# Moving the second query half's compressed softmaxes apart, and a side product behind the items' transposes, in an NSA layer

## The chip, the cores and the metric

The kernel runs on one core of one Trainium2 chip. The time is device microseconds of one execution of the whole program, as the median of several runs. Times inside the program come from one execution that the hardware profiler recorded. Its engines are TensorE (PE), VectorE (DVE), ScalarE (ACT), GpSimd (POOL) and SyncE (SP).

## The reference

A trunk of four layers over 256 tokens of width 1024, all in float32: differential attention, NSA (sparse attention with compressed, selected and window branches), forgetting attention, differential attention again; each layer also has a squared-ReLU MLP and a gated per-layer embedding. The part that matters here is layer 1, the NSA layer:

```python
s_c = einsum('bqgrd,bngd->bgrqn', qc, kc) * scale + b_c     # compressed branch, n_cmp = 15 blocks
p_c = masked_softmax(s_c, m_c)
o_c = einsum('bgrqn,bngd->bqgrd', p_c, vc)
...
s_s, s_w = ...     # scores against the selected and the window keys, 256 of each
p_s, p_w = masked_softmax(s_s, m_s), masked_softmax(s_w, m_w)
return gc[..., 0:1] * o_c + gc[..., 1:2] * o_s + gc[..., 2:3] * o_w
...
x = x + sigmoid(x @ ple_gate_w[i]) * (p[i] @ ple_w[i])      # the embedding; p[i] @ ple_w[i] needs nothing of the layer
```

There are 16 heads in 4 groups. The compressed softmax works on 15 numbers per head and token, so its operations are small, and they form a chain.

## The kernel before, in words

Attention in the NSA layer is cut into 16 **items** `(ap, t, j)`: `ap` is a pair of groups, `t` one of the two token halves of 128, `j` a pair of heads. The order of the items is the table `ORDN`; they are called item 0 to item 15 here. An item has two stages.

- First stage: two score matmuls in two `acc` banks of PSUM (L1005; each shows as two instructions, so a pair is x4), then per row block bias and minimum on DVE (L497), exp on ACT (L501).
- Second stage, three items later (`DP[1]` is 3): on DVE a reciprocal (L1011), the gate (L1013) and four scalings of the probabilities (L1022); on PE transposes into two `wk` banks (L1025), which ACT copies out (L1027), and products with the values into a `pj` bank (L1034), which a matmul with zeros opens where a new `(ap, t)` begins (L1016).

Between the items, `fill(n)` issues other work as the table `FILL` says; it runs after item n-1 has been started and item n-4 has been finished. The letters that matter:

- `s10`: the first part of the compressed softmax of group pair 1, token half 0; `s11` likewise for half 1, and so `s01`, `s00`. It is four small matmuls into a `wk` bank (L959), then a chain: DVE adds the bias (L962 twice), finds the minimum (L966) and subtracts it (L967), ACT takes exp (L968), DVE sums (L970), inverts (L971), applies the gate (L972), and multiplies into `pc` (L976).
- `t00`, `t01`, ...: its second part, four transposes (L982) and a copy by ACT (L983).
- `p`: one step of the embedding's product `ple_proj`: six matmuls of 512 columns in an `acc` bank (L173, L174, L175 twice each) and a copy by ACT (L1145). It depends on nothing in the layer.

Code is written in this order, and a scheduler turns it into one list for each engine; each engine then takes its own list strictly in order. `self.after(x)` holds what is written inside it until `x` stands in the lists. The four `acc` banks are shared by the scores and the embedding; the bias tiles `nb` (two buffers, L486, loaded through ACT's queue) of group pair 1 can be loaded when the last items of pair 0 have used theirs.

Of the kernel before, what the change touches and what calls it, by code (L numbers as in the profile page):

```python
# [18 lines left out]
P = 128  # L19
# [14 lines left out]
PACC = {0: 1, 1: 1, 2: 1, 3: 1}  # L34
PCB = 2
CW = 2
FILL = {-2: 'q0.c.p.q0.c', 1: 'p.g', 2: 'd0.q1.s01.d1', 3: 's00', 4: 't00.q1', 5: 's10.p.s11', 6: 'p', 7: 't01', 11: 't11.t10.O', 16: 'p'}
NORM = {0: 1, 1: 2, 2: 3, 3: 3}
MEP = 1
BANKS = dict(acc=('acc', 4), pj=('pj', 2), wk=('wk', 2))  # L40
# [40 lines left out]
def backwards(v):  # L81

    *rest, (step, n) = [list(z) for z in v.ap]
    return bass.AP(tensor=v.tensor, offset=v.offset + step * (n - 1), ap=[*rest, [-step, n]])


class Trunk:
# [756 lines left out]
    def nsa(self, i, hT):  # L844
        nc, a = self.nc, self.a
# [20 lines left out]
        for t in range(2):  # L866
# [13 lines left out]
            pt = self.wk()  # L880
# [8 lines left out]
        def fill(n):  # L889
            for z in FILL.get(n, "").replace(".", " ").split():  # L890
                if z[0] == "c":
                    if "ph" not in cmp:
                        cmp["ph"] = self.cpsum()
                        cmp["up"] = self.compress_up(blks, cmp["ph"])
                    next(cmp["up"])
                elif z[0] == "g":
                    cmp["hid"] = self.compress_gelu(cmp["ph"])
                elif z[0] == "d":
                    self.compress_down(int(z[1]), cmp["hid"], (kcT, vcd)[int(z[1])])
                elif z[0] == "s":  # L900
                    soft2[z[1:]] = cmp_soft(int(z[1]), int(z[2]), qt[int(z[1])])
                    next(soft2[z[1:]])
                elif z[0] == "t":
                    next(soft2[z[1:]])
                    soft2[z[1:]] = None
                elif z[0] == "q":
                    next(qs[int(z[1])])
                elif z[0] == "p":
                    next(self.ple)
                elif z[0] == "Q":  # L910
                    q_load(int(z[1]))
                elif z[0] == "O":
                    self.early.append(self.unit(self.w_out, len(self.early), 1, 0, D))
            if n > 0:
                for ap, t in last:
                    if (ap, t) in po4 and soft2.get(f"{ap}{t}", 1) is None and n >= last[ap, t] + DP[i]:
                        finish(ap, t)

        qt, po4, soft2 = {}, {}, {}
        last = {(z[0], z[1]): n + 1 for n, z in enumerate(ORDN)}  # L920
        cmp = {}
        blks = [self.compress_blocks(kind, kvT[:, 2 * kind : 2 * kind + 2, :]) for kind in range(2)]
# [4 lines left out]
        def q_load(ap):  # L927
            if ap in q_ws:
                return
            src = w_in[:, 512 * ap : 512 * ap + 512].rearrange("(c p) n -> p c n", p=P)  # L930
            us = q_ws[ap] = []
            for k in range(0, KD, 2):
                w = self.raw(src[:, k : k + 2, :], [4, 4, HD])
                us.append(self.split(w.rearrange("p k r d -> p r k d"), [4, 4, HD]))
# [18 lines left out]
        def cmp_soft(ap, t, qt):  # L953
# [30 lines left out]
            yield  # L984

        fill(-4)
        ksw = self.s4([P, 2, 2, S])
        for z, c in ((0, 512), (1, 1024)):
            o = self.lin_b(w_in, C0 + c, hT)
            nc.scalar.activation(ksw[:, :, z, :], o.rearrange("p (a b) -> p a b", a=2), AF.Copy)  # L990
            fill(z - 3)

        def item(ap, t, j, qt, nbs):


            nk = t + 1
            w = nk * P
            qs = slice(t * P, (t + 1) * P)
            sc = self.acc()
            es = self.es([P, 2, 2, w])  # L1000
            m, s = self.small([P, 4]), self.small([P, 4])
            rows = (j, j ^ 1)
            for g2, r in enumerate(rows):
                hs = slice(g2 * HD, (g2 + 1) * HD)
                nc.tensor.matmul(sc[g2][:, : 2 * w].rearrange("p (z k) -> p z k", z=2), qt[hs, r, qs], ksw[hs, ap, :, :w], start=True, stop=True)  # L1005
            for g2, r in enumerate(rows):
                zs = slice(2 * g2, 2 * g2 + 2)
                self.soft(es[:, g2], lambda b: sc[g2][:, b * w : (b + 1) * w], 2, lambda b: backwards(nbs[g2][:, r, :w]), m[:, zs], s[:, zs])
            for _ in range(DP[i]): yield
            rs = self.small([P, 2, 2])  # L1010
            nc.vector.reciprocal(rs.rearrange("p a b -> p (a b)"), s)  # L1011
            h0, h1 = 8 * ap + rows[0], 8 * ap + 4 + rows[1]
            nc.vector.tensor_tensor(rs, rs, gate[:, t, h0 : h1 + 1 : h1 - h0, 1:3], op=ALU.mult)  # L1013
            if (ap, t) not in po4:
                po4[ap, t] = self.pj()
                nc.tensor.matmul(po4[ap, t], self.zero[0:1, :], self.zero[0:1, 0:1].to_broadcast([1, 512]), start=True, stop=False)  # L1016
            ats = []
            for g2 in range(2):
                e = es[:, g2]
                pt = self.wk()  # L1020
                for z in range(2):
                    nc.vector.tensor_scalar(e[:, z, :], e[:, z, :], rs[:, g2, z : z + 1], None, op0=ALU.mult)  # L1022
                    for kb in range(nk):
                        zz = (z * nk + kb) * P
                        nc.tensor.transpose(pt[:, zz : zz + P], e[:, z, kb * P : (kb + 1) * P], self.ident)  # L1025
                at = self.m2([P, 2, nk, P])
                nc.scalar.activation(at.rearrange("p a b c -> p (a b c)"), pt[:, : 2 * w], AF.Copy)  # L1027
                ats.append(at)
            for z in range(2):
                for kb in range(nk):  # L1030
                    for g2, r in enumerate(rows):
                        g = 2 * ap + g2
                        ov = po4[ap, t][(r % 2) * HD : (r % 2 + 1) * HD, (2 * g2 + r // 2) * P : (2 * g2 + r // 2 + 1) * P]
                        nc.tensor.matmul(ov, vs[kb][:, z, g * HD : (g + 1) * HD], ats[g2][:, z, kb, :], start=False, stop=False)  # L1034

        def finish(ap, t):
            rows = slice(ap * HD, (ap + 1) * HD)
            for g2 in range(2):
                for r in range(4):
                    ov = po4[ap, t][(r % 2) * HD : (r % 2 + 1) * HD, (2 * g2 + r // 2) * P : (2 * g2 + r // 2 + 1) * P]  # L1040
                    nc.tensor.matmul(ov, vcd[rows, 2 * ap + g2, :], pcT[rows, t, r, :], start=False, stop=g2 == 1 and r > 1)
            self.split_out(po4.pop((ap, t)).rearrange("p (a b) -> p a b", a=4), oT, 4 * ap, 4, t)

        def fin():
            for _ in range(DP[i] - 1):
                yield
            fill(100)
            yield

        def items():  # L1050
            n = 0
            nbs = {}
            fill(-1)
            for ap, t, j in ORDN:
                if ap not in nbs:
                    nbs[ap] = [self.bias_load(8 * ap + 4 * g2) for g2 in range(2)]
                yield item(ap, t, j, qt[ap], nbs[ap])
                n += 1
                fill(n)
            yield fin()  # L1060
# [198 lines left out]
```

## Time and profile before

| what | value |
|---|---|
| median of 3 runs | 1384.98 us (1381.73, 1384.98, 1389.02) |
| profiled execution, its own time | 1391.75 us |
| its span, first to last instruction | 1390.0 us |
| PE busy | 1370.6 us, 99% |
| DVE, ACT busy | 906.8 us (65%), 756.9 us (54%) |
| mean granted TensorE clock | 0.991 |

A granted clock of 1.00 is 2.4 GHz and 0.50 is 1.2 GHz. PE is busy nearly all the time, so what PE waits, and what it does at the lower clock, is what a change of order can alter. The stage of the NSA items lies at about 423 to 490 us of the span.

### The profile page before, as it was taken

The page shows a single profiled execution, that of the slowest core. Times are in us where ns is not written, and L with a number is a line of the kernel's source. Part 1 is how long each engine was busy: PE and PEld are TensorE (multiplying, and loading weights), DVE is VectorE, ACT ScalarE, POOL GpSimd, SP SyncE. Part 2 cuts the span into 40 slices and gives each one's busy share as a digit, 9 for nine tenths or more (in the row PEclk, how much of TensorE's full clock was granted, in tenths as well). Part 3 has the DMA queues.
Part 4 walks back from the last instruction along what each step waited for, and adds up shares of the span by engine and source line. Part 5 has one row for each costly group of instructions (what it writes and reads, how often), then busy time and mean ns, then how long its engine had stood idle before and what let it go on. Part 6 is the DMA issues. An engine that isn't in the chain of part 4 may idle for free.

```text
span 1390.0 us, 20343 instructions
## 1 busy us (share of the span) xinstructions
PE 1370.6 (99%) x7604; PEld 1138.5 (82%) x7604; DVE 906.8 (65%) x1636; ACT 756.9 (54%) x1268; POOL 52.9 (4%) x101
## 2 busy tenths in 40 slices
PE   8999999999999999999999999999999999999998
PEld 6987888888875678888878978888888987888887
DVE  6677765667556657656584576766576677766655
ACT  5556554456445755554465575645456566554443
POOL 1011000001000000000010000000001011000000
PEclk9999999999998999999999999999999999999999
DMA  8845765646772036655366644656554753665642
GB/s 267 263 144 154 237 198 188 190 141 195 193 258 95 23 119 223 199 186 183 121 214 197 225 133 154 214 183 198 190 187 124 232 169 102 219 210 170 204 141 76
DMA packets 144526, 247.28 MB, mean 178 GB/s; under 512 B 10195, under 2 KB 101243, under 8 KB 144428
## 3 DMA queue, kind: packets, MB, share of 16 engines
q1 hardware_dynamic: 134848, 235.26, 52.7%
q10 hardware_dynamic: 9580, 10.73, 2.5%
q8 instruction: 60, 0.98, 0.3%
q14 instruction: 38, 0.31, 0.1%
HBM read 243.81 MB, written 1.10 MB: 176 GB/s over the span
## 4 chain that ended last, share of the span: by engine, by line
PE 88%; issue 5%; DVE 2%; ACT 2%; POOL 2%; DMA 1%; SPq 0%; DVEq 0%; POOLq 0%; ACTq 0%
PE pj L182 13%; PE acc L173 13%; PE acc L174 13%; PE acc L175 13%; PE pj L183 7%; PE pj L173 7%; PE pj L175 6%; PE pj L174 6%; PE wk L256 2%; PE acc L627 1%; PE pj L1034 1%; PE acc L1005 1%; PE wk L1025 1%; DMA raw<-in_da_w_in_dram 1%; DVE wl L151 1%
## 5 line engine op out<-in xcount | busy, mean ns | idle before, releaser
L151 DVE TENSOR_TENSOR wl<-raw,wh 128x1024 fp32r<-128x1024 f32 x421 | 510.4, 1221 | 226.7 <-ACT wh L150 215.1
L150 ACT ACTIVATE wh<-raw 128x1024 fp32r<-128x1024 f32 x421 | 443.2, 1058 | 225.5 <-PE acc L174 106.4
L182 PE MATMUL pj<-big,wh 128*128 128x512 f32 x768 | 274.3, 401 | 0.0
L183 PE MATMUL pj<-big,wl 128*128 128x256 f32 x768 | 215.5, 281 | 0.0
L173 PE MATMUL acc<-wh,s 128*128 128x512 f32 x512 | 200.3, 392 | 0.0
L175 PE MATMUL acc<-wl,s 128*128 128x512 f32 x512 | 199.4, 390 | 0.0
L174 PE MATMUL acc<-wh,s 128*128 128x512 f32 x512 | 199.3, 390 | 0.0
L182 PEld LDWEIGHTS pj<-big,wh 128*128 128x128 f32 x768 | 144.2, 188 | 38.2 <-DVE m L1079 3.5
L183 PEld LDWEIGHTS pj<-big,wl 128*128 128x128 f32 x768 | 145.0, 189 | 0.9
L173 PE MATMUL pj<-big,wh 128*128 128x256 f32 x480 | 138.2, 288 | 0.5 <-ACT wh L150 0.5
L174 PE MATMUL pj<-big,wl 128*128 128x256 f32 x480 | 137.0, 285 | 0.5 <-DVE wl L151 0.5
L175 PE MATMUL pj<-big,wh 128*128 128x256 f32 x480 | 137.1, 286 | 0.0
L173 PE MATMUL acc<-wh,big 128*128 128x512 f32 (+2 forms) x344 | 131.6, 383 | 2.3 <-ACT wh L150 2.3
L174 PE MATMUL acc<-wh,big 128*128 128x512 f32 (+2 forms) x344 | 130.7, 380 | 0.0
L175 PE MATMUL acc<-wl,big 128*128 128x512 f32 (+2 forms) x344 | 129.7, 380 | 0.4 <-DVE wl L151 0.4
L175 PEld LDWEIGHTS acc<-wl,s 128*128 128x128 f32 x512 | 96.1, 188 | 20.4
L173 PEld LDWEIGHTS acc<-wh,s 128*128 128x128 f32 x512 | 96.0, 188 | 20.3 <-ACT s L1083 0.3
L174 PEld LDWEIGHTS acc<-wh,s 128*128 128x128 f32 x512 | 96.2, 188 | 19.3 <-DVE s L1084 0.2
L173 PEld LDWEIGHTS pj<-big,wh 128*128 128x128 f32 x480 | 92.4, 193 | 3.1 <-issue 1.2
L174 PEld LDWEIGHTS pj<-big,wl 128*128 128x128 f32 x480 | 92.4, 192 | 2.0 <-DVE wl L151 1.1
L175 PEld LDWEIGHTS pj<-big,wh 128*128 128x128 f32 x480 | 92.4, 192 | 0.4 <-issue 0.2
L501 ACT ACTIVATE s<-s,small 128x128 f32<-128x128 f32 (+1 forms) x160 | 70.8, 446 | 34.2 <-DVE small L497 25.4
(238 smaller groups left out, 1748.1 us busy)
## 6 DMA issues: line engine op xcount, KB each, us to landing
raw<-in_mlp_w_dram SPq DMA_DIRECT2D x256, 512.0 KB, 4.6
raw<-in_da_w_in_dram SPq DMA_DIRECT2D x48, 512.0 KB, 5.3
raw<-in_ple_gate_w_dram SPq DMA_DIRECT2D x32, 512.0 KB, 4.2
raw<-in_fox_w_in_dram SPq DMA_DIRECT2D x24, 512.0 KB, 4.6
raw<-in_nsa_w_in_dram SPq DMA_DIRECT2D x18, 512.0 KB, 4.5
raw<-in_da_w_out_dram SPq DMA_DIRECT2D x16, 512.0 KB, 4.2
g<-in_norm_g_dram SPq DMA_DIRECT2D x15, 512.0 KB, 6.1
nb<-row ACTq DMA_DIRECT2D x12, 512.0 KB, 6.7
```

Of the source, the lines that this page charges most:

```text
L150: self.nc.scalar.activation(wh, w, AF.Copy),
L151: self.nc.vector.tensor_tensor(wl, w, wh.bitcast(F32), op=ALU.subtract),
L173: mm(out, l[0], r[0], start=first, stop=False)
L174: mm(out, l[1], r[0], start=False, stop=False)
L175: self.mms.append(mm(out, l[0], r[1], start=False, stop=last))
L182: mm(out.rearrange("p (z n) -> p z n", z=2), l[0], aT[2][:, :, k, :], start=first, stop=False)
L183: mm(out[:, :S], l[1], a, start=False, stop=last)
L256: z = nc.tensor.transpose(pt[:, c * P : (c + 1) * P], src[:, (b + c) * P : (b + c + 1) * P], self.ident)
L501: nc.scalar.activation(e[:, b, :], e[:, b, :], AF.Exp, bias=m[:, b : b + 1], scale=-1.0, accum_out=s[:, b : b + 1])
L627: self.nc.tensor.matmul(sc[c][:, hh * w : (hh + 1) * w], q[cs, hh, qs], k[cs, hh, :w], start=True, stop=True)
L1005: nc.tensor.matmul(sc[g2][:, : 2 * w].rearrange("p (z k) -> p z k", z=2), qt[hs, r, qs], ksw[hs, ap, :, :w], start=True, stop=True)
L1025: nc.tensor.transpose(pt[:, zz : zz + P], e[:, z, kb * P : (kb + 1) * P], self.ident)
```

## The change

The letter `P` is new: like `p`, but held until the newest transpose of an item (L1025) stands in the lists. In the table, `s10` goes from `fill(5)` to `fill(6)`, `s11` from `fill(5)` to `fill(7)` behind `t01`, and the two steps `p` of the embedding at 5 and 6 become `P` at 5 and 7. Every engine executes the same instructions as before, in another order. Lines from 913 on move down by three: L959 becomes L962, L962 L965, L966 to L968 L969 to L971, L970 to L972 L973 to L975, L976 L979, L982 L985, L1005 L1008, L1011 L1014, L1013 L1016, L1016 L1019, L1022 L1025, L1025 L1028, L1027 L1030, L1034 L1037.

```diff
-FILL = {... 4: 't00.q1', 5: 's10.p.s11', 6: 'p', 7: 't01', 11: 't11.t10.O', 16: 'p'}
+FILL = {... 4: 't00.q1', 5: 'P', 6: 's10', 7: 'P.t01.s11', 11: 't11.t10.O', 16: 'p'}
...
                 elif z[0] == "p":
                     next(self.ple)
+                elif z[0] == "P":
+                    with self.after(turned[-1]):
+                        next(self.ple)
...
-                        nc.tensor.transpose(pt[:, zz : zz + P], e[:, z, kb * P : (kb + 1) * P], self.ident)
+                        turned.append(nc.tensor.transpose(pt[:, zz : zz + P], e[:, z, kb * P : (kb + 1) * P], self.ident))
```

PE's list, before, from the softmax of `s11` on (`s_846` holds the queries of group pair 1, `s_857` the probabilities of item 2, `acc_4327` the embedding's bank, `acc_4356` and `acc_4357` the scores of item 6):

```order
L959 MATMUL wk_4261<-s_708_3283,s_846_3986 128x64 x4
L173 MATMUL acc_4327<-wh_3903,m_799_3796 128x512
L174 MATMUL acc_4327<-wh_3903,m_800_3797 128x512
L175 MATMUL acc_4327<-wl_3904,m_799_3796 128x512
L173 MATMUL acc_4327<-wh_3909,m_799_3796 128x512
L174 MATMUL acc_4327<-wh_3909,m_800_3797 128x512
L175 MATMUL acc_4327<-wl_3910,m_799_3796 128x512
L1005 MATMUL acc_4356<-s_764_3569,s_791_3718 128x512
L1005 MATMUL acc_4357<-s_764_3569,s_791_3718 128x512
L1025 MATMUL wk_4285<-ident_65,s_857_4069 128x128 x4
L1025 MATMUL wk_4294<-ident_65,s_857_4069 128x128 x4
```

PE's list, after, from the softmax of `s10` on (`s_873` holds the probabilities of item 3, `acc_4343` is the embedding's bank):

```order
L962 MATMUL wk_4287<-s_708_3283,s_846_3986 128x64 x4
L1028 MATMUL wk_4309<-ident_65,s_873_4127 128x128 x2
L1028 MATMUL wk_4316<-ident_65,s_873_4127 128x128 x2
L173 MATMUL acc_4343<-wh_3903,m_799_3796 128x512
L1037 MATMUL pj_4105<-m_907_4314,s_712_3294 64x128
```

Six products and a pair of scores stood between a softmax's matmuls and the next item's transposes; now the transposes of item 3 stand directly behind them, and the products behind those. DVE's list, after, at the same place (`mid_4286` is the compressed softmax, `small_4306` the factors of item 3):

```order
L965 TENSOR_TENSOR mid_4286<-wk_4287,s_708_3283 128x60 x2
L969 TENSOR_REDUCE small_4294<-mid_4286 128x8
L970 TENSOR_TENSOR mid_4286<-mid_4286,small_4294 128x120
L973 TENSOR_REDUCE small_4298<-mid_4286 128x8
L1014 RECIPROCAL small_4306<-small_4129 128x4
L974 RECIPROCAL small_4298<-small_4298 128x8
L1016 TENSOR_TENSOR small_4306<-small_4306,s_708_3283 128x4
L975 TENSOR_TENSOR small_4298<-small_4298,s_708_3283 128x8
L1025 TENSOR_SCALAR s_873_4127<-s_873_4127,small_4306 128x128
```

The scalings of an item stand behind the whole chain of one softmax; before, those of item 2 stood behind both. At the second softmax, PE's list after has two pairs of scores between the matmuls and the transposes of item 4 (`s_885`; `acc_4406` and `acc_4407` are item 7's, `acc_4446` and `acc_4447` item 8's):

```order
L962 MATMUL wk_4358<-s_708_3283,s_846_3986 128x64 x4
L1008 MATMUL acc_4406<-s_764_3569,s_791_3718 128x512
L1008 MATMUL acc_4407<-s_764_3569,s_791_3718 128x512
L1008 MATMUL acc_4446<-s_764_3569,s_846_3986 128x512
L1008 MATMUL acc_4447<-s_764_3569,s_846_3986 128x512
L1028 MATMUL wk_4380<-ident_65,s_885_4219 128x128 x4
```

Before, item 7's two score matmuls were apart, with the transposes of item 3 between them, and item 4's transposes came with no softmax ahead.

## Rows read from the trace of the kernel before

**Rows 1.** The page's first part: busy us, share of the span, instructions.

```profile
PE 1370.6 (99%) x7604; PEld 1138.5 (82%) x7604; DVE 906.8 (65%) x1636; ACT 756.9 (54%) x1268; POOL 52.9 (4%) x101
```

**Rows 2.** What PE waited for, 423 to 484 us: us in total, times, longest.

```profile
PE wk L1025 <- DVE s L1022: 1.8, 2, 1.4
PE pj L1034 <- ACT m L1027: 0.3, 1, 0.3
```

**Rows 3.** Stretches: length, busy of PE, PEld, DVE, ACT, POOL, then granted clock.

```profile
436.90:438.40 1.50, 0.10 (x2) 0.08 (x2) 1.44 (x10) 0.22 (x1) 0.00 (x0) 1.00 0.02 5
...
439.20:452.90 13.70, 13.62 (x50) 6.90 (x49) 7.43 (x44) 7.31 (x26) 0.31 (x1) 0.50 0.12 39
...
717.00:719.10 2.10, 0.15 (x1) 0.00 (x0) 0.69 (x1) 0.64 (x2) 1.34 (x2) 1.00 0.94 316
719.10:722.60 3.50, 3.37 (x12) 3.08 (x13) 1.83 (x3) 3.48 (x6) 0.00 (x0) 0.51 0.67 236
```

**Rows 4.** PE's timeline: start, busy, instruction, in brackets the idle time before it.

```profile
424.92 0.30 PE L1025 MATMUL wk<-ident,s 128*128 128x128 f32 x1 [0.42 <-DVE s L1022]
...
428.70 0.39 PE L1016 MATMUL pj<-zero 1*128 1x512 bf16 x1
429.01 0.70 PE L1005 MATMUL acc<-s,s 64*128 64x256 f32 x4
...
432.37 1.33 PE L959 MATMUL wk<-s,s 128*128 128x64 f32 x10
433.51 0.47 PE L173 MATMUL acc<-wh,m 128*128 128x512 f32 x1
...
435.07 1.88 PE L1005 MATMUL acc<-s,s 64*128 64x512 f32 x4
438.36 1.30 PE L1025 MATMUL wk<-ident,s 128*128 128x128 f32 x8 [1.40 <-DVE s L1022]
```

**Rows 5.** DVE's timeline: scalings of item 1, the two softmaxes' chain, scalings of item 2.

```profile
428.37 1.00 DVE L1022 TENSOR_SCALAR s<-s,small 128x128 f32<-128x128 f32 x4
...
433.74 0.22 DVE L962 TENSOR_TENSOR mid<-wk,s 128x60 f32<-128x60 f32 x1 [0.55 <-PE wk L959]
433.88 0.27 DVE L966 TENSOR_REDUCE small<-mid 128x8 f32<-128x120 f32 x1
...
434.19 0.27 DVE L967 TENSOR_TENSOR mid<-mid,small 128x120 f32<-128x120 f32 x1
...
436.50 0.28 DVE L967 TENSOR_TENSOR mid<-mid,small 128x120 f32<-128x120 f32 x1
...
437.23 0.27 DVE L970 TENSOR_REDUCE small<-mid 128x8 f32<-128x120 f32 x1
...
437.86 1.13 DVE L1022 TENSOR_SCALAR s<-s,small 128x256 f32<-128x256 f32 x4
```

**Rows 6.** ACT's timeline: the second softmax's exp, and the load of a bias tile.

```profile
436.81 0.30 ACT L968 ACTIVATE mid<-mid 128x120 f32<-128x120 f32 x1 [0.84 <-DVE mid L967]
...
449.51 0.38 ACTq L486 DMA_DIRECT2D nb<-row  x1
449.99 0.49 ACT L501 ACTIVATE s<-s,small 128x256 f32<-128x256 f32 x1
...
452.61 1.28 ACT L1027 ACTIVATE m<-wk 128x512 f32<-128x512 f32 x2 [1.54 <-PE wk L1025]
```

**Rows 7.** PE's timeline at the full clock: scores as a pair (x4), and alone (x2).

```profile
453.12 1.13 PE L1005 MATMUL acc<-s,s 64*128 64x512 f32 x4
...
456.30 0.70 PE L1005 MATMUL acc<-s,s 64*128 64x256 f32 x2
...
460.77 1.12 PE L1005 MATMUL acc<-s,s 64*128 64x512 f32 x2
```

**Rows 8.** DVE's timeline: bias and minimum of item 7, and of item 8 with the new bias tile.

```profile
447.46 0.42 DVE L497 CUSTOM_DVE_ANT_0 s<-acc,nb 128x256 f32<-128x256 f32 x1 [0.45 <-PE acc L1005]
...
453.23 0.43 DVE L497 CUSTOM_DVE_ANT_0 s<-acc,nb 128x256 f32<-128x256 f32 x1
```

More of the change, by code (lines that the diff above doesn't have):

```diff
@@ L36 @@
 CW = 2
-FILL = {-2: 'q0.c.p.q0.c', 1: 'p.g', 2: 'd0.q1.s01.d1', 3: 's00', 4: 't00.q1', 5: 's10.p.s11', 6: 'p', 7: 't01', 11: 't11.t10.O', 16: 'p'}
+FILL = {-2: 'q0.c.p.q0.c', 1: 'p.g', 2: 'd0.q1.s01.d1', 3: 's00', 4: 't00.q1', 5: 'P', 6: 's10', 7: 'P.t01.s11', 11: 't11.t10.O', 16: 'p'}
 NORM = {0: 1, 1: 2, 2: 3, 3: 3}
@@ L917, in fill @@
                         finish(ap, t)
-        qt, po4, soft2 = {}, {}, {}
+        qt, po4, soft2, turned = {}, {}, {}, []
         last = {(z[0], z[1]): n + 1 for n, z in enumerate(ORDN)}
```

## The prediction

> **What bounds the kernel now.** I read the page's engine shares first: PE is busy 99% of the span, DVE 65%, ACT 54% [rows 1]. So the time is PE's list of work plus what PE waits, and a change that only reorders can move two things: PE's idle time in the stage that it touches, and the clock at which PE works there. Next I asked what PE waited for between 423 and 484 us. Three waits stand there, 2.1 us in all [rows 2]: 0.42 before item 0's transposes, 0.3 before item 1's value products (the row of L1034), and 1.40 before item 2's transposes [rows 4]. The last is the mark that two compressed softmaxes leave: their matmuls end at 433.70 (432.37 + 1.33), the transposes start at 438.36, and the 4.66 us between are covered only by six embedding products (433.51 to 435.07) and item 6's scores (435.07 plus 1.88) [rows 4]. PE must wait for them because DVE takes its list in order, and item 2's scalings stand behind both chains.
>
> Then the stretches. In the wait PE is busy 0.10 of 1.50 us at a granted clock of 1.00; from 439.2 on the clock is 0.50, for 13.7 us in which PE is busy 13.62 [rows 3]. That is 1.2 GHz, so about half of it, 6.8 us, is lost to the clock. Elsewhere a wait of 2 us is followed by a fall too, of 3.5 us, which costs some 1.7 [rows 3]. The two falls differ by 5 us in price, and that is the widest unknown here.
>
> The profiled execution took 1391.75 us, 6.8 above the median of 1384.98. As 6.8 is also the price of the long fall, I take it that the runs near the median lose less of the clock, but no row shows it. I therefore sum differences against the profiled execution and put the sum on the median.
>
> **The change part by part.** Work and instruction counts are the same on every engine, so each term is a wait or an overlap.
>
> *What goes.* The 1.40 before item 2's transposes goes: no softmax stands ahead of them any more, and item 6's first scores do. The 0.3 before item 1's value products goes because an embedding product now stands ahead of them [rows 2]. Together -1.7. The 0.42 at item 0 stays.
>
> *Item 1's transposes.* Before, PE spent the time from 424.92 to 428.70 on item 0's transposes, six products, item 0's value products and the four transposes of a softmax, and after that 0.31 on L1016 (428.70 to 429.01) and 0.70 on item 5's scores [rows 4]. After, the products (1.56, the issue time from 433.51 to 435.07) and the scores stand behind item 1's transposes. So PE arrives at 424.92 + 3.78 - 1.56 + 0.31 = 427.45. DVE's list up to there is the same, and the scalings start at 428.37 [rows 5]; from the first scaling to PE's start it is 0.50 (437.86 to 438.36) [rows 4, 5]. PE starts at 428.87, so +1.4 of new idle time, here or, in part, before item 0's value products, which wait for ACT's copies. Bounds 1.2 to 1.5.
>
> *Item 3's transposes.* The matmuls of `s10` have the transposes directly behind them, and on DVE item 3's scalings stand behind the sum L973, which waits for exp. From rows: end of the matmuls to the first addition 0.04 (433.70 to 433.74); two additions 0.28 (twice 433.74 to 433.88); minimum 0.31 (433.88 to 434.19); subtraction to exp 0.31 (436.50 to 436.81); exp to sum 0.42 (436.81 to 437.23); sum to scalings 0.63 (437.23 to 437.86, with the same four small operations between as after); scalings to PE 0.50 [rows 4 to 6]. That is 2.49 with nothing on PE to cover it: +2.5. The products that used to cover 1.56 of such a chain now stand behind the transposes. Bounds 2.0 (the pieces measured with another softmax's operations between are shorter) to 3.0 (DVE still busy with item 5's minima when the scores of `s10` land).
>
> *Item 4's transposes.* The same chain, with one L497 of item 7 between (0.42) [rows 8], is 2.9; two adjacent pairs of 512-column scores lie on PE in it, 1.06 each (busy 1.13, the last one overlapping) [rows 7]. 2.9 - 2.1 = +0.8. Bounds 0 to 1.2. At half clock the scores take twice as long and the wait is gone.
>
> *The bias load.* The `nb` tile of item 8 is issued on ACT after two exps of item 7 at 449.51, and used 3.72 later, at 453.23 [rows 6, 8]. After, two copies (1.28) and two more exps (0.49 each) stand ahead of it [rows 6]: 2.3 later. Item 8's minima release the banks that the scores of item 10 want at 456.30 [rows 7]; two of the minima take 0.8 of these 3.1 us, which leaves 2.2 of slack. That makes 0.1, or up to 1.1 if other minima stand ahead on DVE; I take +0.5.
>
> *Pairs.* Two score matmuls next to each other take as long as one alone (1.13 for x4, 1.12 for x2 of 512 columns) [rows 7]. In the order of the changed kernel item 7's become adjacent (-1.05) and those of items 10 and 14 (256 columns, 0.63 each after overlap, from 0.70 busy); item 9's are split (+1.05), item 6's (1.88 before, as the second waited for the embedding's bank [rows 4]; +0.2) and item 11's (+0.5). Net -0.5, bounds -1.0 to +0.3.
>
> Sum: 1.4 + 2.5 + 0.8 + 0.5 - 0.5 - 1.7 = +3.0. By the bounds it is +1 to +4.7.
>
> *The clock.* The one idle time of 1.40 that goes was followed by a fall; so was the one of 2.08 near 717 [rows 3, 4]. The new 2.5 is longer than both, so I expect a fall here too, and at the same price: no difference. The Trainium skill speaks of this in "TensorE: Matmul & The Clock Gate", section "What's actually happening": idleness throttles the clock, and sustained activity releases it. The first half agrees with the trace; the second does not in this stage, where 13.62 of 13.70 us busy at 0.50 did not bring the clock back. By that rule a fall in the changed kernel would be short; by the row it may be long again. Both are priced below from rows.
>
> **The rivals.**
> - *The clock falls more (slower).* With waits of 1.4, 2.5 and 0.8 within some 15 us, where before there was one of 1.40, the fall comes in every run, or comes early and lasts longer. For it: the new wait is longer than either wait that the trace shows ahead of a fall. Against it: the profiled execution has its fall already. Price one long fall more than the median run has: 1384.98 + 3.0 + 6.8 = 1394.8. It is beyond 0.5% from a net loss of 6.9 us on.
> - *The stall simply goes (faster).* The chain at item 3 finds cover (DVE ahead of PE by more than the rows say), the 1.7 goes without replacement, and no long fall follows. Then 1384.98 - 1.7 = 1383.3, and down to 1376.5 if the median run had the whole long fall. Against it: nothing stands between matmuls and transposes in PE's list.
> - *The waits come, the fall is short.* +3.0, less the difference of the two falls (6.8 - 1.7 = 5.1): 1382.9. For it: both lengths of fall stand in one trace.
> - *The low clock covers.* The fall starts at item 3, and at half speed the scores cover item 4's chain and the bias load: 3.0 - 0.8 - 0.5 = +1.7, 1386.7.
>
> **How the numbers follow.** Chances: the waits as summed, with the clock as before, 0.50; the clock falling more, 0.23; the stall simply going, 0.09; the short fall, 0.10; the low clock covering, 0.08. The likeliest gives 1384.98 + 3.0 = 1388.0, and by the bounds of its terms 1386 to 1389.7. A measurement here tells about 0.5%, 6.9 us, from no change. Slower by more than that is most of the second case, 0.20; faster by more is the lower part of the third and a little of the fourth, 0.07; the rest, 0.73, is within. The range goes from 1381 to 1396: it leaves out the lower end of the third case and what lies above a whole further fall, together less than 0.2.
>
> **What would show it.** Right, if the waits of PE in this stage name the transposes of item 1 (about 1.4, or shared with item 0's value products), of item 3 (about 2.5, the longest) and of item 4 (below 1.2), all released by DVE's scalings, and the wait before item 2's is gone. Right on the clock, if a stretch at 0.50 begins within 2 us behind the wait at item 3. Wrong, if item 3's wait is below 1.5, or if the stretch at half clock is missing, short, or doubled: then the clock and not the waits decides the result.

## The result, and the profile after

The changed kernel takes 1393.23 us (median of 11 runs, 1387.01 to 1400.67), the kernel before 1384.12 (11 runs). The ratio is 1.0062, 95% interval 1.0045 to 1.0078: slower by 8.6 us by the ratio, where +3.0 was forecast as likeliest. One execution of e2 below, 1488.0 us at a mean clock of 0.849, is left out of all ratios and means (its median is 1389.12 without it). The profiled execution of the changed kernel is the longest of its 11 (1400.67). Its page, first part:

```profile
span 1398.9 us, 20348 instructions
...
PE 1375.8 (98%) x7604; PEld 1139.6 (81%) x7604; DVE 907.1 (65%) x1636; ACT 757.5 (54%) x1268; POOL 51.9 (4%) x101
```

PE is busy 5.2 us longer than before with the same instructions [rows 1], and the rest of the 8.9 us of span is idle time. PE's waits between 423 and 500 us, to be held against [rows 2]:

```profile
PE wk L1028 <- DVE s L1025: 4.6, 4, 2.4
PE acc L1008 <- DVE small L497: 1.1, 2, 0.9
```

PE's timeline at the places of the prediction [rows 4]:

```profile
427.43 0.83 PE L1028 MATMUL wk<-ident,s 128*128 128x128 f32 x4 [0.85 <-DVE s L1025]
...
435.50 1.10 PE L962 MATMUL wk<-s,s 128*128 128x64 f32 x8
439.05 1.31 PE L1028 MATMUL wk<-ident,s 128*128 128x128 f32 x4 [2.44 <-DVE s L1025]
440.01 0.77 PE L173 MATMUL acc<-wh,m 128*128 128x512 f32 x1
...
446.55 1.99 PE L1008 MATMUL acc<-s,s 64*128 64x512 f32 x8
449.40 1.42 PE L1028 MATMUL wk<-ident,s 128*128 128x128 f32 x8 [0.86 <-DVE s L1025]
...
457.12 0.67 PE L1008 MATMUL acc<-s,s 64*128 64x256 f32 x2 [0.22 <-DVE small L497]
458.64 1.72 PE L1008 MATMUL acc<-s,s 64*128 64x512 f32 x2 [0.85 <-DVE small L497]
```

The transposes of items 1, 3 and 4 wait 0.85, 2.44 and 0.86, and the scores wait 0.22 and 0.85 for banks. The 1.40 before item 2's transposes is gone. What comes after two of these waits is seen in stretches, with the columns of [rows 3]:

```profile
438.60:445.40 6.80, 6.35 (x21) 3.94 (x22) 2.62 (x15) 3.03 (x11) 0.00 (x0) 0.50 0.00 0
449.00:459.00 10.00, 8.45 (x61) 4.83 (x62) 6.26 (x34) 6.61 (x23) 0.00 (x0) 1.00 0.34 107
459.00:482.90 23.90, 23.90 (x106) 14.30 (x104) 11.60 (x57) 12.67 (x38) 0.00 (x0) 0.50 0.00 1
```

Two falls of the clock, of 6.8 and 23.9 us: half of 30.7 is 15.4 us lost, against 6.9 by the one fall in this stage before. The second lies behind the bank waits, and in it PE is busy without a gap. Over the whole execution the two profiles differ by less, as that of before has three more falls of 3.4 us outside the stage (near 10, 409 and 720 us) and that of the changed kernel none.

The banks were late because DVE waited for the bias tiles. DVE's timeline:

```profile
448.48 0.42 DVE L497 CUSTOM_DVE_ANT_0 s<-acc,nb 128x256 f32<-128x256 f32 x1
...
450.21 0.42 DVE L497 CUSTOM_DVE_ANT_0 s<-acc,nb 128x256 f32<-128x256 f32 x1
...
455.37 0.42 DVE L497 CUSTOM_DVE_ANT_0 s<-acc,nb 128x256 f32<-128x256 f32 x1 [2.84 <-DMA nb<-row]
...
457.81 0.42 DVE L497 CUSTOM_DVE_ANT_0 s<-acc,nb 128x256 f32<-128x256 f32 x1 [0.83 <-DMA nb<-row]
```

The first two rows are item 7's first and second use of the old bias tile. They stood 0.42 apart before (447.46 in [rows 8] and the next one, below); now item 4's scalings lie between, 1.73 apart. DVE's timeline before, second use:

```profile
447.88 0.42 DVE L497 CUSTOM_DVE_ANT_0 s<-acc,nb 128x256 f32<-128x256 f32 x1
```

In the changed kernel ACT could issue the new load only behind the second use, at 451.38:

```profile
451.38 0.38 ACTq L486 DMA_DIRECT2D nb<-row  x1
```

The second tile's load follows it at 451.79, where before the two stood 3.9 us apart (449.51 and 453.43); it takes 6.0 us from issue to landing, against 4.4 us before. Now both loads are on their way at once, which they hardly were before; what that costs, no run takes apart.

### The profile page after: what moved, and what is told of

It is laid out like the page before. It is cut to its first block, busy times and chain, and to the rows that moved or that the text cites. A ratio compares the mean times of both kernels' runs of the same rounds, so it can differ in the third digit from the quotient of the medians.

```text
span 1398.9 us, 20348 instructions
## 1 busy us (share of the span) xinstructions
PE 1375.8 (98%) x7604; PEld 1139.6 (81%) x7604; DVE 907.1 (65%) x1636; ACT 757.5 (54%) x1268; POOL 51.9 (4%) x101
## 4 chain that ended last, share of the span: by engine, by line
PE 85%; issue 5%; DVE 3%; DMA 2%; ACT 2%; POOL 2%; ACTq 0%; SPq 0%; DVEq 0%; POOLq 0%
PE pj L182 13%; PE acc L173 13%; PE acc L175 13%; PE acc L174 13%; PE pj L183 6%; PE pj L173 6%; PE pj L175 6%; PE pj L174 6%; PE wk L256 2%; DVE wl L151 1%; PE acc L627 1%; PE pj L1037 1%; PE wk L1028 1%; PE acc L1008 1%; DMA raw<-in_da_w_in_dram 1%
```

## Experiments

The theory after the result: the waits are as forecast, and the rest is the clock. Its rival: the waits alone make the loss. Each run lists its mean granted clock, which separates the two: (1 - clock) times the time is what the lower clock took, and what remains is work and waits. The clock is listed to 0.001, 1.4 us, so only means over many runs are used. The split is an estimate: PE's last matmul ends 4.9 us before the end of the span, and a low clock there costs it nothing; where PE would wait anyway, a low clock costs less than it says. Among the runs of before, the time rises by 0.7 to 0.8 us for each us of this loss, among the 11 of the changed kernel by 1.2. So 1 to 2 us may stand in the wrong column. It also counts the falls outside the stage, none to three in a profiled run.

| kernel | ratio to before (95%) | clock's loss | against its before | remainder against its before |
|---|---|---|---|---|
| changed | 1.0062 (1.0045 to 1.0078) | 10.3 | +6.0 | +2.1 |
| e1 plain p | 1.0022 (1.0003 to 1.0041) | 7.2 | +2.9 | +0.3 |
| e2 P alone | 1.0020 (1.0003 to 1.0037) | 5.3 | +1.0 | +2.0 |
| e3 bias on SP | 1.0082 (1.0062 to 1.0102) | 12.3 | +8.0 | +3.3 |
| e4 products late | 1.0034 (1.0022 to 1.0047) | 7.1 | +2.8 | +1.8 |
| e5 second p | 1.0047 (1.0019 to 1.0076) | 10.4 | +5.0 | +2.5 |
| e6 plain, late | 1.0006 (0.9995 to 1.0016) | 7.0 | +1.7 | -1.4 |
| e7 before, late | 0.9983 (0.9972 to 0.9994) | 4.4 | -1.0 | -1.5 |
| e8 cover both, late | 0.9997 (0.9985 to 1.0008) | 6.9 | +1.5 | -2.6 |
| e9 s11 at 8 | 1.0012 (0.9997 to 1.0027) | 5.2 | +0.4 | +1.4 |
| e10 before, at 13 | 0.9996 (0.9977 to 1.0014) | 6.7 | +1.9 | -2.1 |

All in us, means over 6 to 12 runs of the kernel. The kernel before, run beside: loss 4.3 and remainder 1380.9 with e1 to e4 (29 runs, also used for the changed kernel, as the runs of before in its own comparison have no clock on record), 5.4 and 1379.1 with e5 to e8 (35 runs), 4.8 and 1380.1 with e9 and e10 (23 runs). The standard error of a loss is 0.4 to 1.2, of e5's 2.0; that of a remainder 0.3 to 0.8.

**e1, both P as p.**

```diff
-5: 'P', 6: 's10', 7: 'P.t01.s11'
+5: 'p', 6: 's10', 7: 'p.t01.s11'
```

> The changed kernel with the letter P written p again, so that only the softmaxes are moved and the products are free to stand early. In PE's list the second step's six products and item 7's scores then stand between the matmuls of s10 and item 3's transposes (1.56 + 1.06 = 2.6 against the chain of 2.5), and the first step's products stand ahead of item 1's transposes as before the change. Waits theory: the waits of 0.85 (item 1), 2.44 (item 3) and 0.86 (item 4) fall to below 0.5 each; 4 us gone, time about 1389 if the clock stays as in the changed kernel. Clock theory: with no wait over 1.4 us ahead, the fall at item 3 goes too and the time lies at or below the kernel before, 1381 to 1385. Rival, the late bias load alone makes the second, longer fall: then the wait before item 10's scores (1.07) and a long stretch at 0.50 behind it stay, and the time is 1388 to 1391.

Median 1387.83. The three waits behind the softmaxes are gone, as both theories say; the bank wait is 1.5:

```profile
PE acc L1008 <- DVE small L497: 1.5, 1, 1.5
PE pj L1037 <- ACT m L1030: 0.9, 3, 0.3
PE wk L1028 <- DVE s L1025: 0.4, 1, 0.4
```

The remainder is that of before, and the clock still takes 2.9 us more. The clock theory's figure of at most 1385 missed; the rival that it named, the late bias load, is near (1388 to 1391): in the profiled run the only fall of this stage begins at 446.9, behind the wait of 1.5. It lasts 6.8 us, against 23.9 in the changed kernel:

```profile
445.15 1.12 PE L1008 MATMUL acc<-s,s 64*128 64x512 f32 x2 [1.55 <-DVE small L497]
```

```profile
446.90:453.70 6.80, 6.80 (x27) 3.65 (x26) 2.60 (x14) 2.83 (x8) 0.00 (x0) 0.50 0.43 130
```

By this run the hold by `P` is what added the +2 of waits; e5, which takes off one of the two holds, doesn't show its share.

**e2, P in the places of before.**

```diff
-5: 'P', 6: 's10', 7: 'P.t01.s11'
+5: 's10.P.s11', 6: 'P', 7: 't01'
```

> The letter P in the places of the kernel before (5: s10.P.s11, 6: P, 7: t01), so that the products are held behind the transposes and the softmaxes stay together. The two chains of 4.9 us are then covered only by item 5's scores (0.7), a pair of 256 columns. Waits theory: item 2's transposes wait about 3 to 3.5 us instead of 1.40, item 1's about 0.85; no chain ahead of items 3 and 4, no late bias load; about +2.5 on the kernel before, 1386.5. Clock theory: a fall behind the wait at item 2, but six products right behind it, as after the wait at item 3 in the changed kernel, so a stretch of some 7 us and no second one: 1384 to 1388. If the time is 1392 or more, the softmaxes' places have no part in the loss.

Median 1389.18. The longest wait of any run, 2.85, with products right behind it:

```profile
433.15 0.70 PE L1008 MATMUL acc<-s,s 64*128 64x256 f32 x4
436.70 1.61 PE L1028 MATMUL wk<-ident,s 128*128 128x128 f32 x8 [2.85 <-DVE s L1025]
437.96 0.77 PE L173 MATMUL acc<-wh,m 128*128 128x512 f32 x1
```

and a fall of only 3.4 us, after which the clock stays up:

```profile
437.10:440.50 3.40, 3.40 (x14) 1.89 (x12) 2.31 (x15) 2.69 (x10) 0.00 (x0) 0.50 0.01 2
440.50:480.00 39.50, 39.50 (x289) 23.87 (x289) 25.17 (x134) 29.16 (x99) 0.31 (x1) 1.00 0.09 28
```

The waits are as expected (+2.0), and the loss to the clock is 1.0 above before, though the wait is the longest. So a fall's price doesn't follow the length of the wait.

**e3, bias tiles of pair 1 through SyncE.**

```diff
-nbs[ap] = [self.bias_load(8 * ap + 4 * g2) for g2 in range(2)]
+nbs[ap] = [self.bias_load(8 * ap + 4 * g2, "as"[ap]) for g2 in range(2)]
```

> The changed kernel with the two bias tiles of group pair 1 loaded through SyncE's queue instead of ACT's, so that their issue doesn't stand behind ACT's copies and exps. Waits theory: only the wait before item 10's scores (1.07) goes, about -1 us, 1392. Clock theory: with that wait the second fall (0.50 for 23.9 us in the profiled run, some 12 us lost) goes, so -4 to -6 in the median, 1387 to 1389, and the profile shows one stretch at half clock, behind item 3's wait. Rival: the second fall comes from the sum of waits from item 3 on; then it stays, and the time is 1391 to 1394.

Median 1396.15, and the clock theory's figure missed. What PE waited for:

```profile
PE wk L1028 <- DVE s L1025: 4.6, 4, 2.4
PE acc L1008 <- DVE small L497: 0.5, 2, 0.3
```

The bank wait halved, but DVE waited 3.0 us for the tiles all the same. The first load was issued 0.8 us earlier (450.55 against 451.38), right behind the release of the old tile, and its tile was used no earlier (455.45 against 455.37): from issue to use it took 4.9 us instead of 4.0. So taking ACT's queue away gained nothing on the first tile; why the load took longer, no run tells. A long fall still begins at 459.1, behind 0.26 and 0.22 of bank waits and 0.86 at item 4:

```profile
459.10:472.80 13.70, 13.70 (x59) 8.24 (x58) 7.48 (x40) 6.82 (x25) 0.00 (x0) 0.50 0.00 1
```

So shortening this wait by half doesn't keep the clock. The run doesn't tell why the remainder rose to +3.3.

**e4, the last products at 10.** This moves the fourth step of the embedding to where the long fall begins.

```diff
-7: 'P.t01.s11', 11: 't11.t10.O', 16: 'p'
+7: 'P.t01.s11', 10: 'p', 11: 't11.t10.O'
```

> The changed kernel with the last step of the embedding (the p at 16) moved to 10, so that its six products of 512 columns stand where the second fall begins. All else of the table as changed. Waits theory: no difference beyond 1 us, 1392 to 1394. Clock theory, that the items' own small matmuls don't bring the clock back and the products do: the wait before the scores stays at about 1, the clock still falls there, but the stretch at 0.50 behind it is below 9 us instead of 23.9, and the median is 1386 to 1389. If the stretch stays above 18 us with the products at its start, what the engine does there doesn't decide its length.

Median 1389.91. The same waits stand ahead (2.44, 0.86), then waits of 0.38 ahead of the products and 0.44 between the fifth and the sixth:

```profile
457.67 0.50 PE L173 MATMUL acc<-wh,m 128*128 128x512 f32 x1 [0.38 <-DVE small L497]
...
458.70 0.40 PE L174 MATMUL acc<-wh,m 128*128 128x512 f32 x1
459.55 1.15 PE L1028 MATMUL wk<-ident,s 128*128 128x128 f32 x8 [0.44 <-DVE s L1025]
```

```profile
440.50:447.30 6.80, 6.80 (x26) 4.61 (x25) 1.47 (x8) 3.94 (x12) 0.46 (x2) 0.50 0.00 0
457.60:482.00 24.40, 23.80 (x182) 15.25 (x184) 20.45 (x103) 22.49 (x74) 0.00 (x0) 1.00 0.14 44
```

The second fall doesn't come in this execution. The remainder is as with the changed kernel (+1.8, against +2.1), and 3.2 us of clock come back: the loss is at most 8.4 us in any of 12 runs, where the changed kernel has runs of 15.4. So the clock theory is borne out in the mean, though its median of 1386 to 1389 was missed by 0.9, and in the profile the fall stays away instead of being short. That the products kept it away is argued: e5 and e7 have an execution without a fall behind waits of 1.55 and 1.40, with no products close behind.

**e5, the first P kept, the second as p.**

```diff
-7: 'P.t01.s11'
+7: 'p.t01.s11'
```

> The changed kernel with only the second P (at 7) written p again: the products of that step stand right behind s10's matmuls and, with item 7's scores, ahead of item 3's transposes; the first P (at 5) stays, and so does the wait before item 1's transposes. Waits theory: 0.85 stays, 2.44 and 0.86 fall below 0.3, a wait for a score bank of 1 to 1.5 stays (the bias tile comes late as with plain p): full-clock time 1.5 to 2 below the changed kernel's. Clock theory: the only wait over 1 us is that for the bank, so a fall only there; mean clock about 0.995 as with plain p, and 1386 to 1389. If the mean clock stays at 0.993, item 3's wait isn't what lowers it.

Median 1389.09, item 3's wait gone, the bank wait 1.5:

```profile
PE acc L1008 <- DVE small L497: 1.5, 1, 1.5
PE wk L1028 <- DVE s L1025: 1.3, 2, 0.8
PE pj L1037 <- ACT m L1030: 0.3, 1, 0.3
```

The mean clock stays at 0.993: by the expectation, item 3's wait isn't what lowers it, with 2.0 us of standard error on a loss of +5.0. The loss has two groups: 1.4 to 8.3 us in 7 runs, 16.8 to 21.0 in 5. The profiled run is of the first and shows no fall in the stage, so what a long one looks like here wasn't seen. The remainder (+2.5) should have been some 1.5 below the changed kernel's and wasn't; with two groups of so few runs I draw nothing from that.

**e6, e1 and e4 together.**

```diff
-5: 'P', 6: 's10', 7: 'P.t01.s11', 11: 't11.t10.O', 16: 'p'
+5: 'p', 6: 's10', 7: 'p.t01.s11', 10: 'p', 11: 't11.t10.O'
```

> The softmaxes in the places of the changed kernel, both P written p, and the last step of the embedding at 10 instead of 16: the two edits that each gave back some of the loss together. If they add (plain p -5.4 us, late products -3.3 us), the time is 1384 to 1386 with a mean clock of 0.996 or more. If plain p already leaves nothing for the late products to repair, it is as with plain p, 1387 to 1388.5.

Median 1384.99, the time of before within the interval. The time is back, in a kernel that has the softmaxes in the changed places, but not by the clock: its loss is 7.0 us, as with e1 alone (7.2), and still 1.7 above before; the mean clock of 0.996 that was expected was 0.995. What fell against e1 is the remainder, from +0.3 to -1.4, as it does in e7 and e10, where the same step leaves its place at 16.

**e7, the kernel before with the last products at 10.**

```diff
-5: 's10.p.s11', 6: 'p', 7: 't01', 11: 't11.t10.O', 16: 'p'
+5: 's10.p.s11', 6: 'p', 7: 't01', 10: 'p', 11: 't11.t10.O'
```

> The kernel before with only the last step of the embedding moved from 16 to 10. The wait of 1.40 before item 2's transposes stays. Waits theory: no difference beyond 0.1%. Clock theory: a long stretch at half clock, which in the kernel before some executions show (0.990 to 0.994 in 3 of 29), is cut short by products that come some 20 us behind the wait; the mean clock goes from 0.997 to 0.998 and the median by -0.5 to -1.5 us.

Median 1381.90: faster than both kernels by a little (0.9983). But most of the gain is in the remainder (-1.5), which the clock theory didn't expect; the clock's -1.0 is about one standard error. The wait of 1.4 is still there, and in this execution no fall follows it in the stage:

```profile
PE wk L1028 <- DVE s L1025: 1.4, 1, 1.4
PE pj L1037 <- ACT m L1030: 0.5, 2, 0.3
```

**e8, both softmaxes covered, last products at 10.**

```diff
-5: 's10.p.s11', 6: 'p', 7: 't01', 11: 't11.t10.O', 16: 'p'
+5: 's10.p.s11.p', 7: 't01', 10: 'p', 11: 't11.t10.O'
```

> The opposite of the change: both softmaxes stay together at 5, the second step of the embedding is moved up to them (5: s10.p.s11.p), so that item 6's scores and item 5's stand between the softmaxes' matmuls and item 2's transposes, and the last step is at 10. Waits theory: with 1.56 of products gone from behind the softmaxes, the wait before item 2's transposes grows to some 3 us unless PE is later there by those products; as they stand ahead of item 1's transposes, PE comes 1.6 later, DVE is further ahead, and the sum of the waits is 0.5 to 2 us below that of the kernel before. Time 1382 to 1384.5 if the clock is as before; with a fall behind a wait of 3 us it is 1386 or more.

Median 1383.65, no difference from before. The expectation on the waits missed: PE waits 2.6 us in the stage, 0.5 more than before and not 0.5 to 2 less. The remainder is the lowest of all (-2.6) even so; as in e7 and e10, the last step has left its place at 16. The clock takes 1.5 more: the wait before item 2's transposes is 2.0 with no products behind it, and the profiled run shows a fall of 10.2 us there.

**e9, s11 behind item 7's first stage.** The counterpart of e5: the longest wait stays, and those behind it go.

```diff
-7: 'P.t01.s11'
+7: 'P.t01', 8: 's11'
```

> The changed kernel with s11 at 8 instead of 7: item 7's scores and minima come ahead of the second softmax, so the bias tiles are free earlier and neither item 4's transposes nor a score bank is waited for; the wait of 2.4 before item 3's transposes, with the products right behind it, stays, and so does item 1's 0.85. It is the counterpart of the run with only the second P as p, which removed item 3's wait and kept the bank's. If the late bank wait, with nothing but the items' small matmuls behind it, causes the loss of clock: mean clock 0.996 (some 5 us lost instead of 10), no stretch at half clock behind 446 us in the profile, 1385.5 to 1388. If the longest wait, item 3's, causes it: mean clock 0.993 and 1390 to 1393.

Median 1386.79. PE's waits, the last of them before item 5's transposes, and the stretch behind item 3's:

```profile
PE wk L1028 <- DVE s L1025: 4.2, 4, 2.4
```

```profile
452.17 1.18 PE L1028 MATMUL wk<-ident,s 128*128 128x128 f32 x4 [0.44 <-DVE s L1025]
```

```profile
439.60:443.00 3.40, 3.40 (x14) 1.86 (x13) 2.70 (x15) 2.85 (x10) 0.00 (x0) 0.50 0.00 0
443.00:482.00 39.00, 38.16 (x293) 24.14 (x292) 25.98 (x145) 28.97 (x98) 0.46 (x2) 1.00 0.09 29
```

No bank wait, no fall behind 443, and the time and clock of the expectation's first branch. A wait of 0.44 remains with only small matmuls behind it, and no fall follows it here. The clock's loss is 0.4 above before, in all 12 runs between 0.995 and 0.999 of clock. Moving one softmax by one item gives back nearly all that the clock took in the changed kernel, with the longest wait unchanged.

**e10, the kernel before with the last products at 13.**

```diff
-11: 't11.t10.O', 16: 'p'
+11: 't11.t10.O', 13: 'p'
```

> The kernel before with the last step of the embedding at 13 instead of 16 (the run at 10 gave 0.9983 of the time of before). If the gain at 10 comes from the clock, by products that end a stretch at half clock, a place 10 to 15 us later gives less: ratio 0.9985 to 1.0005. If it comes from a cost that the step has at its old place at the end of the layer's items, it is the same at 13: 0.9975 to 0.999, with the same gain in the time less the clock's loss, about 1.5 us.

Median 1383.74. By its ratio (0.9996) this is the expectation's first branch, by its remainder the second: the remainder falls as in e7 (-2.1), which points to a cost at the step's old place at 16. Which cost, no run shows, and e4, where the step leaves 16 too, doesn't have the gain (+1.8, against +2.1 of the changed kernel). The clock's loss (6.7 against 4.4 at 10) points to the earlier place as the better for the clock, but the standard errors (0.8 for e7) and the wide interval don't settle it.

## Why the prediction was right and wrong

The direction was right, 1393.2 lies in the range of 1381 to 1396, and the outcome was not the likeliest case but the rival "the clock falls more", at 0.23. To a time slower by more than 6.9 us, as this one is by 8.6, the prediction gave 0.20. Point by point:

- *What goes.* Right: the waits before item 2's transposes and item 1's value products are gone from the list.
- *Item 1's transposes.* The start was right (3.88 us behind item 0's first transposes, 423.55; forecast 3.95). The idle time was 0.85 instead of 1.4: the item's other work ends at 426.58, so taking the products out shortened that piece by 1.06 and not by their 1.56.
- *Item 3's transposes.* 2.44, forecast 2.5; the chain added up from single rows holds.
- *Item 4's transposes.* 0.86, forecast 0.8.
- *The bias load.* 1.07, forecast 0.5 with 1.1 as upper bound. The mechanism was wrong: not ACT's copies ahead of the issue, but DVE's list, where item 4's scalings hold up the last use of the old tile. e3 took ACT's queue away, and DVE still waited 3.0 us for the tile.
- *Pairs.* No run separates the forecast -0.5.
- *The sum of waits.* In the profiled executions PE's waits grow by 3.5 us (0.85 + 2.44 + 0.86 + 1.07 - 1.40 - 0.32), and the terms without the pairs forecast the same 3.5. That is partly luck: the forecast was 0.55 too high for item 1 and 0.57 too low for the bias load. In the remainder it is +2.1, forecast +3.0. The stated bounds of +1 to +4.7 are narrower than the bounds of the terms, which add up to +0.6 to +5.4.
- *The clock.* This is the step that failed: "I expect a fall here too, and at the same price: no difference". The lower clock took 6.0 us more, and the prediction's own sign of being wrong came, a stretch at half clock that is doubled (13.7 before, 30.7 after). The base was wrong too: the profiled execution of before, with its fall of 13.7 us, is not typical; 26 of 29 runs beside e1 to e4 have a mean clock of 0.995 or more, the profiled one 0.991. That its 6.8 above the median equals the price of its long fall is chance, as three more falls stand outside the stage.

The rival's size was near (1394.8 against 1393.2), but the wait that it rested on was the wrong one. e9 keeps the 2.4 and the clock is as before; e5 removes it and the loss stays; e2 has 2.85 and loses 1.0. What the costly cases have in common (the changed kernel, e3, e5, and e1 with less) are waits of 0.2 to 1.5 us after about 445, where the embedding's products are past and PE's list holds only the items' small matmuls and transposes. e4 puts six products there and loses 3.2 us less. So the reading that fits is that the place of a wait sets the price: what PE has to do behind it. The profiled executions agree only in part. Behind waits of 2.4 to 2.9 with products right behind, the falls last 3.4 to 6.8 us (the changed kernel, e2 to e4, e9). With no products close behind they last 23.9 (the changed kernel), 13.7 (before, e3, e10), 10.2 (e8) or 6.8 us (e1), and in e5, e7 and e9 none comes. So the reading is argued, not shown. The Trainium skill, in "TensorE: Matmul & The Clock Gate", section "HAM oscillation — how this bites in real kernels", tells of waits for DMA behind which the next burst of matmuls starts at the lower clock. Here bank waits below 1 us stand ahead of a fall of 23.9 us, and PE was busy in all of it.

Open stays which of the two later waits starts the second fall in the changed kernel, that at item 4 or the one for the banks. e1 and e5 keep only the bank's and lose clock; e3 has half of it and item 4's, and loses it too; e9 has neither, only 0.44 at item 5. Shown is that `s11` at 7 is the cause of most of the clock's loss, as e9 differs from the changed kernel in that alone (+0.4 against +6.0); that it acts through these two waits is argued. Why a fall without products lasts 6.8 us in one run and 23.9 in another, no run tells.

## What to carry to other kernels

When a change moves waits, sum them from rows, and then ask of each one, however small, what the engine does behind it: here a wait of 2.9 us with large matmuls behind it cost little, and moving one softmax, by which waits of 0.86, 0.22 and 0.85 with only small matmuls behind them gave way to one of 0.44, gave back most of the clock's loss. Moving large matmuls that depend on nothing into a long stretch of small ones is worth a try: it gave back 3.2 us of that loss in e4, and nothing clear in e6. One profiled execution may not be the typical one: the mean clock of every run, split into its loss and a remainder, told the two causes roughly apart where the times alone could not.

## What was not expected of the hardware

PE at 1.2 GHz and busy 23.90 of 23.90 us did not get its full clock back for 23.9 us, with matmuls of 64x512, 64x256 and 128x128 in its list; with six matmuls of 128x512 within the first 6 us behind a wait of 2.4 to 2.9, falls lasted 3.4 to 6.8 us (the changed kernel, e2 to e4, e9), one execution of each. One run of e5 lost 21.0 us to the clock by its mean, some 42 us at half clock over the whole execution, in one fall or several.
